# A decoder trunk on one core: where the Conformer's norm is multiplied in, where six key pieces stand, and how layer-norm sums are issued

## The chip, the cores and the metric

The kernel runs on one core of one Trainium2 chip. The metric is the time of one launch in microseconds, taken on the device; the number compared is the median of several runs. Profiles are of one execution each.

## The reference

The model is a trunk of two layers on 512 positions with 1024 channels, in single precision, with cross-attention into 256 memory tokens. Layer 0 is a recurrent and pooling mixer, then cross-attention, then a gated feed-forward net with a causal convolution of width 3. Layer 1 is a Conformer convolution module, then cross-attention and a feed-forward net again. The change lies between the first feed-forward net and the second cross-attention, so it is these lines that matter:

```python
def rms_norm(x, g):
    return x * lax.rsqrt(jnp.mean(x * x, axis=-1, keepdims=True) + EPS) * g

def conformer_conv(x, norm, w1, b1, dw_w, dw_b, ln_g, ln_b, w2, b2):
    h = rms_norm(x, norm) @ w1 + b1            # 1024 -> 2048
    h = jax.nn.glu(h, axis=-1)                 # a * sigmoid(b)
    h = causal_dwconv(h, dw_w, dw_b)           # 31 taps
    h = jax.nn.silu(layer_norm(h, ln_g, ln_b)) # mean and variance over channels
    return h @ w2 + b2

# the second attention's keys depend on the memory alone:
m = rms_norm(mem, mem_norm); k = m @ wk; v = m @ wv
```

## The kernel before

**Layout.** Activations lie with channels on the 128 partitions: `X` is eight tiles of 128x512 (channel block c, all positions). A weight of 1024x1024 is eight pieces of 128x1024, and a piece serves one output block: eight 128x128 blocks, one for each input block.

**Products.** Single precision is made of three products in a reduced format: `mm3` (L158, L159, L160) multiplies high by high, high by low and low by high parts. So an output block of 512 columns is 8 x 3 = 24 matmuls, and one of the memory's 256 columns as well. `load_w` loads a piece by DMA on SyncE (`raw`, three buffers), makes its high part `whi` on ScalarE (L152) and its low part `wlo` by a subtraction on VectorE or, for the Conformer's `pieces` and the values, on GpSimd (L153, `eng=G`). `whi` and `wlo` have four buffers each, so a piece's parts are made when the piece four before it has been used up. `split` does the same for an activation: high part on ScalarE, low part on VectorE.

**Order.** Each engine runs its instructions in a fixed order, which a tile scheduler derives from the order of the code, priorities (`load_w` runs ahead by `AHEAD`), and `issue_after` marks. The whole trunk is one stream of matmuls on TensorE.

**Two ways to apply an RMS norm.** `Norm.feed` (L176 to L185) takes each block as it is finished, multiplies it by the gain alone into an operand's high and low part, and adds up squares. The positions' factor r = 1/sqrt(mean + eps) is only known when all blocks are; whoever uses the product multiplies by r afterwards. `Scaled` only adds up squares in `feed`; `scale()` makes r (`rstd`: a sum over partitions by two matmuls L216, L217, a square root on ScalarE L237, a reciprocal on VectorE L239), and `split(c)` then multiplies block c by gain and r (L209) and splits the product. Before, the Conformer's norm `n3` is a `Norm`.

**The Conformer.** `glu(c)` makes output block c of the two halves: 24 matmuls for the sigmoid's half `psb`, 24 for `psa`, the multiplications by r (L676, L680), the sigmoid (L677), and their product `h` (L683). Four DMAs on SyncE (L690) copy h into a stacked form for the convolution on TensorE. `conv_pe(c)` computes some of the 31 taps by matmuls against diagonal weights, which GpSimd writes just before (L705); the matmuls are L711, and there are 3 groups of 4 taps for the blocks 0 to 6 and 8 groups for block 7. `conv(c)` adds the other taps on VectorE (L729), ScalarE and GpSimd (L727). `quarters` (L223) sums finished blocks over channels for the layer norm: four matmuls of full single precision into four 32-row strips, called after every fourth block for the mean (`mu`) and again for the variance (`var`). Then r, the multiplications L774, the activation, and the second projection `pw2`.

**Keys of the second attention.** `mem.keys(n)` is one weight piece against the memory's 256 columns: 24 matmuls of 256 columns. It depends on nothing in the trunk, and is used as filler. Five of the eight (`KE = 5`) stand in the first feed-forward net, two in each of the steps g = 2 and 3 and one in g = 4, behind `down(g - 1)`. Number 5 stands in the Conformer before `conv_pe(7)`, and numbers 6 and 7 behind the values in the layer norm.

Of the kernel before, what the change touches and what calls it, by code (L numbers as in the profile page):

```python
# [12 lines left out]
AF = mybir.ActivationFunctionType  # L13
ALU = mybir.AluOpType
# [4 lines left out]
C = D // P  # L19
# [12 lines left out]
N_POOL = [4] * 7 + [0]  # L32
LAG = 5

KE = 5
WINDOWS = (2, 4, 8, 16)


# [16 lines left out]
def trunk(ctx: ExitStack, tc: tile.TileContext, I: dict, out: bass.AP):  # L55
    nc = tc.nc
    V, A, G, PE = nc.vector, nc.scalar, nc.gpsimd, nc.tensor
# [14 lines left out]
    def nm(s):  # L72
        uid[0] += 1
        return f"{s}_{uid[0]}"
# [13 lines left out]
    def tmp_f(n=T):  # L88
        return tmp.tile([P, n], F32, tag="tmp", name=nm("tmp"))
# [26 lines left out]
    def col(name, i=0):  # L116
        j = _COL[name] + i
        return par[:, j : j + 1]

    onesf = cpool.tile([P, P], F32, tag="onesf", name="onesf")  # L120
# [16 lines left out]
    def load_w(src=None, eng=None, raw=None, parts=1):  # L137
        with tc.high_priority(0 if raw is not None else AHEAD):
            if raw is None:
                raw = wp.tile([P, D], F32, tag="raw", name=nm("raw"), bufs=3)  # L140
                nc.sync.dma_start(raw, src)
            hi = wp.tile([P, D], F32R, tag="whi", name=nm("whi"))
            lo = wp.tile([P, D], F32R, tag="wlo", name=nm("wlo"))
            n = D // parts
            for i in range(0, D, n):
                split(raw[:, i : i + n], hi[:, i : i + n], lo[:, i : i + n], eng)
        return hi, lo

    def split(src, hi=None, lo=None, eng=None):
        hi = act_r() if hi is None else hi  # L150
        lo = act_r() if lo is None else lo
        A.activation(hi, src, AF.Copy)  # L152
        (eng or V).tensor_tensor(lo, src, hi.bitcast(F32), op=ALU.subtract)  # L153
        return hi, lo
# [67 lines left out]

    def quarters(ps, xs):  # L223

        for j in range(4):
            n = len(xs) - 4 + j
            PE.matmul(ps[32 * j : 32 * j + 32], onesf[:, :32], xs[n], start=n < 4, stop=n >= 4)  # L227

    def total(ps, out):
        f = tmp_f()  # L230
# [11 lines left out]
    def project(w, i, xs):  # L242
        ps = mm_ps()
        for k in range(C):
            mm3(ps, blk(w, k * P), xs[k], k == 0, k == C - 1)
        if Norm.due:
            Norm.due.r = rstd(Norm.due.ss)
            Norm.due = None
        return ps
# [172 lines left out]
    def ffn(layer, norm, nxt, mem=None):  # L422
        ys = {}

        def up(c):
            ps = project(load_w(I["wup"][(layer * 2) * CF + c]), c, norm.x)
            g = tmp_f(T + 2)
            G.memset(g[:, :2], 0.0)  # L428
            V.tensor_tensor(g[:, 2:], ps, norm.r, op=ALU.mult)  # L429
            y = tmp_f()  # L430
            dw = lambda j: col("f_dw_w", (layer * 3 + j) * CF + c)
            A.activation(y, g[:, 2:], AF.Identity, scale=dw(2), bias=col("f_dw_b", layer * CF + c))  # L432
            for j in (1, 0):
                V.scalar_tensor_tensor(y, g[:, j : j + T], dw(j), y, op0=ALU.mult, op1=ALU.add)  # L434
            A.activation(y, y, AF.Gelu_apprx_tanh)  # L435
            G.tensor_tensor(y, y, norm.r, op=ALU.mult)  # L436
            ps = project(load_w(I["wup"][(layer * 2 + 1) * CF + c]), c, norm.x)
            V.tensor_tensor(y, ps, y, op=ALU.mult)  # L438
            ys[c] = split(y)

        def down(g):
            for j in range(C // 2):
                w = load_w(I["wdown"][(layer * NG + g) * (C // 2) + j])
                for i in range(2):
                    n = 2 * j + i
                    ps = mm_ps()
                    for k in range(GC):
                        mm3(ps, blk(w, k * 2 * P + i * P), ys[g * GC + k], k == 0, k == GC - 1)
                    V.tensor_tensor(X[n], X[n], ps, op=ALU.add)  # L449
                    if g == NG - 1:  # L450
                        nxt.feed(n)

        for g in range(NG):
            for c in range(g * GC, (g + 1) * GC):
                up(c)
            if g:
                down(g - 1)
                if mem and g == 1:
                    mem.operand(0)
                    mem.operand(1)  # L460
                    mem.outputs()
                for n in range(2 * g - 4, 2 * g - 2):
                    if mem and 0 <= n < KE:
                        mem.keys(n)
        if nxt:
            down(NG - 1)
        else:
            finish([ys[(NG - 1) * GC + k] for k in range(GC)])
# [196 lines left out]
    def conformer(norm, nxt, mem):  # L665
# [7 lines left out]
        def glu(c, w):  # L673
            psb = project(w[0], c, norm.x)
            b = tmp_f()
            V.tensor_tensor(b, psb, norm.r, op=ALU.mult)  # L676
            A.activation(b, b, AF.Sigmoid, bias=col("c_b_pw1", C + c))  # L677
            psa = project(w[1], c, norm.x)
            a = tmp_f()
            V.tensor_tensor(a, psa, norm.r, op=ALU.mult)  # L680
            h = tmp.tile([P, T + 4], F32, tag="h", name=nm("h"), bufs=3)
            G.memset(h[:, :4], 0.0)
            V.scalar_tensor_tensor(h[:, 4:], a, col("c_b_pw1", c), b, op0=ALU.add, op1=ALU.mult)  # L683
            stacked = [act_f() for _ in range(4)]
            for j in range(4):

                v = h[32 * j : 32 * j + 32, 1 : 1 + T].unsqueeze(1).broadcast_to([32, 4, T])
                dims = [list(d) for d in v.ap]
                dims[1][0] = 1
                nc.sync.dma_start(stacked[j], bass.AP(v.tensor, v.offset, dims))  # L690
            hs[c] = h[:, 4:], stacked
# [58 lines left out]
        for c in range(C):  # L750
            if c < C - 1:
                glu(c + 1, w)
            if c == C - 1:
                mem.keys(KE)
            conv_pe(c)
            if c < C - 2:
                w = pieces(c + 2)
            elif c == C - 1:
                mem.eng = G
                ready = [mem.piece(i) for i in range(3)]  # L760
            conv(c)
# [10 lines left out]
        xs = []  # L772
# [5 lines left out]
        with tc.issue_after(late.ins):  # L778
            mem.values(0, ready)
            mem.values(1)  # L780
            for n in range(KE + 1, C):
                mem.keys(n)
        for n in range(C):
            ps = project(load_w(I["pw2"][n], G), n, xs)
# [5 lines left out]
    mem = Memory(0, load=False)  # L790
# [19 lines left out]
    for n in range(C):  # L810
        mem.keys(n)
        n0.split(n)
    n1, n2, n3 = Norm(("xa_norm", 0)), Norm(("f_norm", 0)), Norm(("c_norm", 0))
    n4, n5 = Norm(("xa_norm", C)), Norm(("f_norm", C))
    mixer(n0, n1)
    attention(0, n1, mem, n2)
    mem = Memory(1)
    ffn(0, n2, n3, mem=mem)
    conformer(n3, n4, mem)
    attention(1, n4, mem, n5)  # L820
    ffn(1, n5, None)


# [65 lines left out]
```

## Time and profile before

| what | us |
|---|---|
| median of three runs | 1503.77 (1503.7 to 1505.58) |
| profiled execution, its own time | 1505.68 |
| its span | 1503.9 |
| TensorE busy | 1481.5 (99%) |
| VectorE / ScalarE / GpSimd busy | 936.2 / 636.5 / 216.6 |

In the trace of before the feed-forward net's last down projection ends near 775, the GLU runs from there to near 883, the layer norm to near 939, and the second projection follows. How to read the rows below: the first number is the start in us from the span's start, the second the duration; then engine, line, operation, output<-inputs, shape and count, and in brackets the time for which the engine stood idle before it and whose end released it. Each row of TensorE with `xN` is N records in a row; a convolution or layer-norm sum in full single precision leaves two records for each instruction.

### The profile page before, as it was taken

To read this page: it belongs to the slowest core of one execution; us is meant where nothing else is said; L and a number is where in the kernel's file an instruction comes from. 1 tells how busy PE (TensorE), PEld (TensorE's weight loads), DVE (VectorE), ACT (ScalarE), POOL (GpSimd) and SP (SyncE) were. 2 spreads that over 40 slices of the span, in tenths; PEclk is the share of its full clock that TensorE was granted. 3 is DMA by queue.
4 is the path that set the end of the run, shared out by engine and by line. 5 is a ranking of instruction groups with operands and counts; after the bars stand their busy time and mean duration, and the time that the engine had idled before them with its cause. 6 is when DMAs were issued, how large, how long until landed. Compare 5 with 4: busy or idle time off the path is not lost.

```text
span 1503.9 us, 17839 instructions
## 1 busy us (share of the span) xinstructions
PE 1481.5 (99%) x6974; PEld 1210.1 (80%) x6974; DVE 936.2 (62%) x1222; ACT 636.5 (42%) x878; POOL 216.6 (14%) x226
## 2 busy tenths in 40 slices
PE   8999999999999999999999999999999999999997
PEld 7888788888888888888877665888888888888886
DVE  7987765656554555555566996866665554545556
ACT  7578744444432333333253336544443332323333
POOL 0011300000110101000036763300001010101000
PEclk9999999999999999999999999999999999999998
DMA  7432332213333332333326542331233333323321
GB/s 273 149 108 85 121 118 97 71 31 124 98 98 98 96 107 94 111 98 105 94 81 169 158 141 94 103 94 57 71 98 98 98 98 98 98 96 92 97 81 57
DMA packets 47477, 156.24 MB, mean 104 GB/s; under 512 B 5280, under 2 KB 7328, under 8 KB 47392
## 3 DMA queue, kind: packets, MB, share of 16 engines
q1 hardware_dynamic: 46160, 154.03, 33.1%
q8 instruction: 55, 0.90, 0.2%
q10 hardware_dynamic: 1232, 1.06, 0.2%
q14 instruction: 30, 0.25, 0.1%
HBM read 144.58 MB, written 2.10 MB: 98 GB/s over the span
## 4 chain that ended last, share of the span: by engine, by line
PE 89%; DVE 5%; issue 2%; ACT 2%; POOL 1%; DMA 1%; SPq 0%; DVEq 0%; POOLq 0%; ACTq 0%
PE mm L159 27%; PE mm L158 27%; PE mm L160 27%; PE aux L711 2%; PE aux L160 1%; PE aux L159 1%; PE aux L158 1%; DVE wlo L153 1%; ACT whi L152 1%; DVE act L177 1%; POOL tmp L569 1%; PE aux L372 0%; DVE r L239 0%; DVE actf L774 0%; PE aux L227 0%
## 5 line engine op out<-in xcount | busy, mean ns | idle before, releaser
L159 PE MATMUL mm<-act,whi 128*128 128x512 f32 (+1 forms) x1845 | 712.8, 387 | 3.1 <-DVE act L153 1.9
L160 PE MATMUL mm<-act,wlo 128*128 128x512 f32 (+1 forms) x1845 | 712.5, 386 | 1.6 <-DVE wlo L153 1.6
L158 PE MATMUL mm<-act,whi 128*128 128x512 f32 (+1 forms) x1845 | 712.4, 387 | 0.7 <-ACT act L176 0.5
L152 ACT ACTIVATE whi<-raw 128x1024 fp32r<-128x1024 f32 x267 | 282.7, 1060 | 617.0 <-PE mm L159 460.8
L159 PEld LDWEIGHTS mm<-act,whi 128*128 128x128 f32 x1845 | 347.4, 188 | 77.0 <-issue 3.3
L160 PEld LDWEIGHTS mm<-act,wlo 128*128 128x128 f32 x1845 | 347.3, 188 | 73.7 <-DVE wlo L153 2.4
L158 PEld LDWEIGHTS mm<-act,whi 128*128 128x128 f32 x1845 | 347.5, 188 | 72.0 <-ACT act L176 1.0
L153 DVE TENSOR_TENSOR wlo<-raw,whi 128x1024 fp32r<-128x1024 f32 x233 | 288.0, 1238 | 60.5 <-ACT whi L152 60.0
L436 POOL TENSOR_TENSOR tmp<-tmp,r 128x512 f32<-128x512 f32 x48 | 62.0, 1292 | 652.0 <-ACT tmp L435 647.1
L449 DVE TENSOR_TENSOR x<-x,mm 128x512 f32<-128x512 f32 x88 | 60.4, 687 | 99.8 <-PE mm L160 99.8
L429 DVE TENSOR_TENSOR tmp<-mm,r 128x512 f32<-128x512 f32 x48 | 33.2, 692 | 124.1 <-PE mm L160 124.1
L153 POOL TENSOR_TENSOR wlo<-raw,whi 128x1024 fp32r<-128x1024 f32 x34 | 82.8, 2435 | 114.4 <-ACT whi L152 114.4
L438 DVE TENSOR_TENSOR tmp<-mm,tmp 128x512 f32<-128x512 f32 x48 | 33.2, 691 | 95.5 <-POOL tmp L428 80.9
L729 DVE SCALAR_TENSOR_TENSOR aux<-h,par,aux 128x496 f32<-128x496 f32 (+14 forms) x105 | 75.1, 728 | 8.2 <-PE aux L711 6.0
L153 DVE TENSOR_TENSOR act<-tmp,act 128x512 fp32r<-128x512 f32 x102 | 73.3, 723 | 5.9 <-ACT act L152 5.7
L152 ACT ACTIVATE act<-tmp 128x512 fp32r<-128x512 f32 x102 | 63.8, 628 | 26.4 <-DVE tmp L185 7.6
L434 DVE SCALAR_TENSOR_TENSOR tmp<-tmp,par,tmp 128x512 f32<-128x512 f32 x96 | 71.9, 749 | 1.7
L435 ACT ACTIVATE tmp<-tmp 128x512 f32<-128x512 f32 x48 | 30.3, 632 | 95.1 <-DVE tmp L434 95.1
L428 POOL MEMSET tmp<- 128x2 f32 x48 | 4.6, 99 | 300.0 <-DVE tmp L185 300.0
L177 DVE SCALAR_TENSOR_TENSOR act<-x,par,act 128x512 fp32r<-128x512 f32 x40 | 40.2, 1008 | 8.0 <-ACT act L176 8.0
L432 ACT ACTIVATE tmp<-tmp,par 128x512 f32<-128x512 f32 x48 | 38.6, 805 | 0.6 <-DVE tmp L429 0.6
L239 DVE RECIPROCAL r<-tmp 128x512 f32<-128x512 f32 (+1 forms) x10 | 28.7, 2872 | 15.5 <-ACT tmp L237 15.5
(195 smaller groups left out, 1234.8 us busy)
## 6 DMA issues: line engine op xcount, KB each, us to landing
raw<-in_wup SPq DMA_DIRECT2D x96, 512.0 KB, 3.5
raw<-in_wdown SPq DMA_DIRECT2D x48, 512.0 KB, 3.5
raw<-in_pw SPq DMA_DIRECT2D x24, 512.0 KB, 3.6
raw<-in_win SPq DMA_DIRECT2D x20, 512.0 KB, 3.6
raw<-in_wv SPq DMA_DIRECT2D x16, 512.0 KB, 4.8
raw<-in_wk SPq DMA_DIRECT2D x16, 512.0 KB, 3.9
raw<-in_wq SPq DMA_DIRECT2D x16, 512.0 KB, 3.6
raw<-in_wo SPq DMA_DIRECT2D x16, 512.0 KB, 3.6
```

What stands on the lines that cost most here:

```text
L152: A.activation(hi, src, AF.Copy)
L153: (eng or V).tensor_tensor(lo, src, hi.bitcast(F32), op=ALU.subtract)
L158: PE.matmul(ps, wh, xh, start=first, stop=False)
L159: PE.matmul(ps, wh, xl, start=False, stop=False)
L160: PE.matmul(ps, wl, xh, start=False, stop=last)
L177: self.last = V.scalar_tensor_tensor(lo, X[c], g, hi.bitcast(F32), op0=ALU.mult, op1=ALU.subtract)
L429: V.tensor_tensor(g[:, 2:], ps, norm.r, op=ALU.mult)
L432: A.activation(y, g[:, 2:], AF.Identity, scale=dw(2), bias=col("f_dw_b", layer * CF + c))
L434: V.scalar_tensor_tensor(y, g[:, j : j + T], dw(j), y, op0=ALU.mult, op1=ALU.add)
L436: G.tensor_tensor(y, y, norm.r, op=ALU.mult)
L449: V.tensor_tensor(X[n], X[n], ps, op=ALU.add)
L729: V.scalar_tensor_tensor(ps[:, s:], h[:, : T - s], tap(s, c), ps[:, s:], op0=ALU.mult, op1=ALU.add)
```

## The change

There are three edits. The first makes `n3` a `Scaled`, and moves keys: none are left in the feed-forward net, two stand behind it, two behind the making of r, one after four of the operand's blocks and one after all eight; `KE` is 6, so that numbers 6 and 7 stay where they were. The second follows from it: `glu` needs no factor r, so the sigmoid and the product read PSUM. The third marks three of the four matmuls of `quarters` to be issued after the one that is created first, which takes the last of the four blocks.

```diff
     def quarters(ps, xs):
-        for j in range(4):
+        def quarter(j):
             n = len(xs) - 4 + j
-            PE.matmul(ps[32 * j : 32 * j + 32], onesf[:, :32], xs[n], start=n < 4, stop=n >= 4)
+            return PE.matmul(ps[32 * j : 32 * j + 32], onesf[:, :32], xs[n], start=n < 4, stop=n >= 4)
+
+        with tc.issue_after(quarter(3).ins):
+            for j in range(3):
+                quarter(j)
...
-                for n in range(2 * g - 4, 2 * g - 2):
-                    if mem and 0 <= n < KE:
-                        mem.keys(n)
...
             b = tmp_f()
-            V.tensor_tensor(b, psb, norm.r, op=ALU.mult)
-            A.activation(b, b, AF.Sigmoid, bias=col("c_b_pw1", C + c))
+            A.activation(b, psb, AF.Sigmoid, bias=col("c_b_pw1", C + c))
             psa = project(w[1], c, norm.x)
-            a = tmp_f()
-            V.tensor_tensor(a, psa, norm.r, op=ALU.mult)
...
-            V.scalar_tensor_tensor(h[:, 4:], a, col("c_b_pw1", c), b, op0=ALU.add, op1=ALU.mult)
+            V.scalar_tensor_tensor(h[:, 4:], psa, col("c_b_pw1", c), b, op0=ALU.add, op1=ALU.mult)
...
-            if c == C - 1:
-                mem.keys(KE)
             conv_pe(c)
...
-            for n in range(KE + 1, C):
+            for n in range(KE, C):
                 mem.keys(n)
...
-    n1, n2, n3 = Norm(("xa_norm", 0)), Norm(("f_norm", 0)), Norm(("c_norm", 0))
+    n1, n2, n3 = Norm(("xa_norm", 0)), Norm(("f_norm", 0)), Scaled(("c_norm", 0))
...
     ffn(0, n2, n3, mem=mem)
+    mem.keys(0)
+    mem.keys(1)
+    n3.scale()
+    mem.keys(2)
+    mem.keys(3)
+    for c in range(C):
+        n3.split(c)
+        if c % 4 == 3:
+            mem.keys(4 + c // 4)
     conformer(n3, n4, mem)
```

Later lines move by a few numbers: what was L239 is L244 after the change, L306 (the keys' product with the memory's factor) L311, L683 is L682, L711 is L710. TensorE has the same number of instructions as before, VectorE eight fewer.

The order on VectorE where the Conformer begins, before. `x` are the channel blocks, `mm_6069` the last down product, `act` the parts of the operand, `r_6139` the factor, `h` the first GLU blocks:

```order
L449 TENSOR_TENSOR x<-x,mm_6069 128x512
L177 SCALAR_TENSOR_TENSOR act_6084<-x,par,act_6083 128x512
L185 TENSOR_TENSOR tmp_6089<-tmp_6067,tmp_6087 128x512
L153 TENSOR_TENSOR act_6131<-tmp_6089,act_6130 128x512
L239 RECIPROCAL r_6139<-tmp_6137 128x512
L676 TENSOR_TENSOR tmp_6141<-mm_6105,r_6139 128x512
L680 TENSOR_TENSOR tmp_6169<-mm_6144,r_6139 128x512
L683 SCALAR_TENSOR_TENSOR h_6171<-tmp_6169,par,tmp_6141 128x512
```

The same place after the change, from the reciprocal on. `bigr` are parts of the keys, `mm_5964` and `mm_5999` key products:

```order
L244 RECIPROCAL r_5956<-tmp_5954 128x512
L311 TENSOR_TENSOR tmp_5989<-mm_5964,r_271 128x256
L311 TENSOR_TENSOR tmp_6024<-mm_5999,r_271 128x256
L209 SCALAR_TENSOR_TENSOR tmp_6028<-x,par,r_5956 128x512
L153 TENSOR_TENSOR bigr_3951<-tmp_5989,bigr_3950 128x256
L153 TENSOR_TENSOR bigr_3951<-tmp_6024,bigr_3950 128x256
L209 SCALAR_TENSOR_TENSOR tmp_6034<-x,par,r_5956 128x512
L153 TENSOR_TENSOR act_6031<-tmp_6028,act_6030 128x512
L209 SCALAR_TENSOR_TENSOR tmp_6040<-x,par,r_5956 128x512
L209 SCALAR_TENSOR_TENSOR tmp_6046<-x,par,r_5956 128x512
L153 TENSOR_TENSOR act_6037<-tmp_6034,act_6036 128x512
```

Between the reciprocal and the first `h` VectorE now has 24 instructions (eight L209, eight splits of them, four key products and four splits of those) where it had two.

On TensorE, keys 0 and 1, the two statistic matmuls and keys 2 to 5 stand in this order ahead of GLU 0. The two halves of GLU 0 are not one after the other: ten products of `psb` come first, then single or a few products of `psa` and `psb` in turn, and last thirteen of `psa`, so that the eighth operand block is first asked for late among the 48.

The order on TensorE at the last convolution block, before. `aux_6990` is block 6, `aux_7068` block 7; the `mm_7231` and `mm_7232` rows are the second attention's values:

```order
L160 MATMUL mm_7039<-bigr_3940,wlo_7036 128x256
L227 MATMUL stat_6182<-actf_6771,onesf 32x512
L158 MATMUL mm_7231<-whi_7107,bigr_3930 128x512
...
L160 MATMUL mm_7232<-whi_7107,bigr_3931 128x512
L711 MATMUL aux_6990<-actf_6861,actf_6991 32x512
...
L711 MATMUL aux_6990<-actf_6864,actf_6991 32x504
L158 MATMUL mm_7231<-whi_7113,bigr_3930 128x512
...
L159 MATMUL mm_7231<-wlo_7120,bigr_3940 128x512
L711 MATMUL aux_7068<-actf_6982,actf_7069 32x512
```

After the change, `aux_7010` is block 6 and `aux_7053` block 7; `mm_6974` is the last GLU product, `mm_7216` and `mm_7217` are values:

```order
L160 MATMUL mm_6974<-act_6107,wlo_6916 128x512
L158 MATMUL mm_7216<-whi_7092,bigr_3930 128x512
...
L159 MATMUL mm_7217<-wlo_7099,bigr_3930 128x512
L710 MATMUL aux_7010<-actf_6884,actf_7011 32x512
...
L710 MATMUL aux_7010<-actf_6887,actf_7011 32x504
L710 MATMUL aux_7053<-actf_7002,actf_7054 32x512
```

The key piece (`mm_7039`) and the layer-norm sum are gone from here; 17 value matmuls stand between the last GLU product and block 6 (12 before, behind the key piece), and none between block 6 and block 7, where there were 20.

For the blocks 1 to 5 the convolution of block c stood four matmuls into the `psa` half of GLU c+2. Block 1, before (`mm_6436` is the end of `psb` of GLU 3, `mm_6464` the start of its `psa`, `aux_6381` the convolution):

```order
L160 MATMUL mm_6436<-act_6083,wlo_6399 128x512
L158 MATMUL mm_6464<-act_5913,whi_6404 128x512
L159 MATMUL mm_6464<-act_5914,whi_6404 128x512
L160 MATMUL mm_6464<-act_5913,wlo_6405 128x512
L158 MATMUL mm_6464<-act_5933,whi_6404 128x512
L711 MATMUL aux_6381<-actf_6253,actf_6382 32x512
```

After the change, block 0 shows what now holds for all of them (`mm_6353` is `psb` of GLU 2, `aux_6299` the convolution):

```order
L160 MATMUL mm_6353<-act_6089,wlo_6317 128x512
L158 MATMUL mm_6353<-act_6095,whi_6316 128x512
L159 MATMUL mm_6353<-act_6096,whi_6316 128x512
L710 MATMUL aux_6299<-actf_6215,actf_6300 32x512
```

The convolution of block c now stands 17 matmuls into `psb` of GLU c+2, eleven earlier than before for the blocks 1 to 5.

More of the change, by code (lines that the diff above doesn't have):

```diff
@@ L33 @@
 LAG = 5
-KE = 5
+KE = 6
 WINDOWS = (2, 4, 8, 16)
```

## The prediction

> **What bounds the kernel now.** I read the page's engine line first, then the busy time by stretch, then the rows of TensorE around the places that the change touches.
>
> ```profile
> PE 1481.5 (99%) x6974; PEld 1210.1 (80%) x6974; DVE 936.2 (62%) x1222; ACT 636.5 (42%) x878; POOL 216.6 (14%) x226
> 500.00:600.00 100.00, 100.00 (x465) 83.81 (x464) 54.22 (x66) 33.45 (x40) 7.99 (x12) 1.00 0.32 100
> 755.00:784.00 29.00, 26.47 (x107) 20.73 (x106) 20.29 (x22) 14.67 (x21) 11.68 (x5) 0.94 0.29 85
> 784.00:905.00 121.00, 120.04 (x647) 80.90 (x646) 102.29 (x137) 43.32 (x56) 77.78 (x59) 1.00 0.54 150
> 905.00:945.00 40.00, 38.44 (x162) 24.02 (x158) 25.37 (x34) 28.44 (x40) 14.56 (x6) 0.96 0.25 79
> ```
>
> TensorE is busy for 99% of the span. The other rows give the stretch, its length, the busy time of TensorE, of its weight loads, VectorE, ScalarE and GpSimd, and the granted clock. In the feed-forward net, where five key pieces now stand, no gap is left, so they hide nothing there and leave without cost. The change issues the same matmuls as before, so its effect lies in gaps and half-clock periods, and the three other stretches hold 2.53, 0.96 and 1.56 us of gaps.
>
> First the boundary to the Conformer:
>
> ```profile
> 769.67 0.39 PE L160 MATMUL mm<-act,wlo 128*128 128x512 f32 x1
> ...
> 774.43 0.39 PE L160 MATMUL mm<-act,wlo 128*128 128x512 f32 x1
> 775.37 0.49 PE L158 MATMUL mm<-act,whi 128*128 128x512 f32 x1 [0.55 <-ACT act L176]
> 777.09 0.50 PE L159 MATMUL mm<-act,whi 128*128 128x512 f32 x1 [1.23 <-DVE act L177]
> ...
> 779.67 0.63 PE L158 MATMUL mm<-act,whi 128*128 128x512 f32 x1
> ...
> 782.24 0.52 PE L158 MATMUL mm<-act,whi 128*128 128x512 f32 x1
> 931.18 0.28 PE L158 MATMUL mm<-bigr,whi 128*128 128x256 f32 x1
> ...
> 936.81 0.28 PE L160 MATMUL mm<-bigr,wlo 128*128 128x256 f32 x1
> 939.39 0.71 PE L159 MATMUL mm<-act,whi 128*128 128x512 f32 x1 [1.45 <-DVE act L153]
> ...
> 942.89 0.42 PE L158 MATMUL mm<-act,whi 128*128 128x512 f32 x1
> ```
>
> Starts count, since records overlap. From 769.67 to 774.43 are 21 steps of 0.227 us. These 21 matmuls are the first seven blocks of GLU 0, so the last down projection ends one step behind 769.67, at E = 769.9. Then the eighth block's parts are late, made by ScalarE and VectorE, and after these gaps six matmuls, 779.67 to 782.24, run at 0.43 us each: the clock was halved. Key matmuls of 256 columns take 0.12 us (47 steps from 931.18 to 936.81), so a key piece is 24 x 0.12 = 2.9 us.
>
> **The change part by part.** A plus is time added.
>
> *What the boundary loses now.* From E to 782.24 are 12.3 us, in which 24 + 6 products and two statistic matmuls run: 32 x 0.227 = 7.3. It loses 5.1 us, and with keys as cover all of that can go: **-5.1**.
>
> *What the boundary gets.* After E come keys 0 and 1 (to E+5.8), two statistic matmuls (E+6.3), and keys 2 to 5 (E+17.9). Then GLU 0 wants the new operand, one of eight blocks each three matmuls, and ends its `psb` 5.4 us and both halves 10.9 us later, at E+28.8 if nothing is late. When are the blocks there?
>
> ```profile
> 779.96 1.28 ACT L237 ACT_TABLE_LOAD   x1 [0.71 <-PE stat L217]
> 781.25 0.69 ACT L237 ACTIVATE tmp<-stat,eps 128x512 f32<-128x512 f32 x1
> 781.97 3.35 DVE L239 RECIPROCAL r<-tmp 128x512 f32<-128x512 f32 x1 [2.95 <-ACT tmp L237]
> 47.73 0.74 DVE L209 SCALAR_TENSOR_TENSOR tmp<-x,par,r 128x512 f32<-128x512 f32 x1
> 48.39 0.42 DVE L306 TENSOR_TENSOR tmp<-mm,r 128x256 f32<-128x256 f32 x1
> 48.72 0.74 DVE L209 SCALAR_TENSOR_TENSOR tmp<-x,par,r 128x512 f32<-128x512 f32 x1
> 49.38 0.68 DVE L153 TENSOR_TENSOR act<-tmp,act 128x512 fp32r<-128x512 f32 x1
> 49.98 0.42 DVE L153 TENSOR_TENSOR bigr<-tmp,bigr 128x256 fp32r<-128x256 f32 x1
> 50.32 0.68 DVE L153 TENSOR_TENSOR act<-tmp,act 128x512 fp32r<-128x512 f32 x1
> ```
>
> The statistic is there at E+6.4; the table load and square root take 1.28 + 0.69 us behind some ScalarE work on a weight piece (about 0.8), so to E+9.2, and the reciprocal 3.35, to E+12.5. The rows from 47.73 on, of the first layer, show the same building of an operand between keys: from start to start 0.66 us for L209, 0.60 for its split, 0.33 for a key product and 0.34 for that one's split. Eight, eight, four and four of them are 13 us, one after the other on VectorE: the last block stands at about E+25.5, a block every 1.6 us from E+14. TensorE asks for the first block at E+17.9, when it is done, and then for a new one every 1.4 us, as the order takes both halves of GLU 0 in turn. Putting these times into the order, matmul by matmul, I get gaps of 0.1 us in sum.
>
> What speaks for a larger loss is that two engines' instructions hold each other:
>
> ```profile
> 945.54 5.20 POOL L153 TENSOR_TENSOR wlo<-raw,whi 128x1024 fp32r<-128x1024 f32 x2 [10.36 <-ACT whi L152]
> 946.01 2.48 DVE L153 TENSOR_TENSOR act<-tmp,act 128x512 fp32r<-128x512 f32 x1 [0.77 <-ACT act L152]
> 948.41 2.61 DVE L153 TENSOR_TENSOR bigr<-tmp,bigr 128x256 fp32r<-128x256 f32 x1
> L683 DVE SCALAR_TENSOR_TENSOR h<-tmp,par,tmp x8: 751/1888/2669, 789.6 to 884.6; 128x512 f32<-128x512 f32 x8
> ```
>
> While GpSimd split two pieces, a VectorE split that takes 0.68 took 2.48, and one that takes 0.42 took 2.61: each ended with a GpSimd instruction. The eight L683, minimum, median and maximum in ns, vary from 751 to 2669 for the same reason. Three GpSimd splits of Conformer pieces (the second of GLU 0 and both of GLU 1, 2.4 us or more each) come due in the window from E+12.5, since their buffers come free as the keys' pieces are used up. Nearly every VectorE instruction there reads two tensors of SBUF (x and r, or a product and its high part). With three holds, each from the start of a split that falls on a waiting VectorE instruction, the same exercise puts the low parts of blocks 0, 1 and 3 to E+20.7, 22.7 and 27.4 and the last to E+32.4. TensorE then waits 2.7, 1.3 and 2.8 us for the three and 0.5 for others: 7.2, and GLU 0 ends at E+36.0, not 28.8. At the half clock that such gaps leave, the products between them take 0.43, which fills part of the later gaps but lengthens the end: 8.3 to 9.3. I take **+8.9**; the ends are 0.1 and 9.3.
>
> The Trainium skill, "SBUF — State Buffer", section "Who interferes with whom", states that a VectorE instruction with two SBUF inputs contends with a GpSimd instruction that reads SBUF, and that the one that comes first has the shared ports for its whole instruction. The rows of 945.54 to 948.41 agree. By the same page the new `h`, which reads PSUM and one SBUF tensor, is no longer held; that is off TensorE's path except for the waits below.
>
> *Queues.* Six key pieces of 512 KB in 18 us are 175 GB/s on SyncE's queue; the stretch from 784 on moves 150 at a share of 0.54, so that is 0.63, and I cost it at nothing. ScalarE and VectorE split them ahead of the reciprocal, at 1.1 and 1.2 us for each 2.9 of TensorE; the bound above nothing is one late piece, the 1.2.
>
> *Convolutions.* `conv_pe(c)` now stands 17 matmuls (3.9 us) behind the end of `psa` of GLU c+1; for c = 1 to 5 it was 28 (6.4 us).
>
> ```profile
> 811.40 1.06 ACT L152 ACTIVATE whi<-raw 128x1024 fp32r<-128x1024 f32 x1 [3.38 <-PE mm L159]
> 812.54 2.41 POOL L153 TENSOR_TENSOR wlo<-raw,whi 128x1024 fp32r<-128x1024 f32 x1 [3.07 <-ACT whi L152]
> 814.91 1.29 POOL L705 TENSOR_TENSOR actf<-fold,par 128x384 f32<-128x384 f32 x1
> 801.29 0.85 POOL L705 TENSOR_TENSOR actf<-fold,par 128x384 f32<-128x384 f32 x1
> ```
>
> The taps are made on GpSimd behind the split of a piece whose high part waits for TensorE to use up `psa`'s piece: 1.06 + 2.41 + 0.85 = 4.3 and some 0.1 between, 4.4 us. So TensorE waits about 0.55 at each of six blocks, 3.3 in sum. The whole stretch from 784 to 905 has 0.96 us of gaps now, of which I put 0.2 to these places: **+3.1**. With 1.29 for the taps the waits would be 1.0 each, +5.8; if the pieces are split before this, 0.
>
> *Sums.*
>
> ```profile
> 914.18 1.47 PE aux L227 x4
> 916.31 0.97 PE aux L227 x2
> 918.18 0.97 PE aux L227 x2
> 920.75 0.98 PE aux L227 x4
> 885.84 1.05 PE L227 MATMUL stat<-actf,onesf 128*32 128x512 f32 x2
> 898.20 6.89 PE L711 MATMUL aux<-actf,actf 128*32 128x512 f32 x64 [0.24 <-DVE actf L738]
> ```
>
> A group takes 0.97 us whether it is one instruction (x2 records) or two, since the strips run side by side. Before, the order has eleven groups; after, five (one is still split in 3 and 1). One of the six saved lies ahead of the last GLU product: **-1.0**. The other five count in the tail, next.
>
> *The tail.* Before the sum at 885.84 stand the 24 matmuls of key number 5, 2.9 us, so the last GLU product ends at Q = 882.9. From there to the first `pw2` matmul, whose wait ends at 939.39, are 56.5 us. Number 5 leaves (it was paid for at the boundary): 53.5. Five groups fewer are 4.9, and the tail's gaps of today (1.56 and 0.24 by the rows above, and some more) about 2.1: TensorE has 46.5 us to do. But the convolution of block 7 started at 898.20, Q+15.3, behind number 5, a sum, 32 value products and block 6. Now 17 value products (3.9), a wait of 0.55 and block 6 (24 records against 64 in 6.89 us, 2.6) are ahead of it: Q+7.0. It needs the copies of h.
>
> ```profile
> 887.02 4.28 SPq L690 DMA_DIRECT2D actf<-h  x4
> DMA to landing us min/median/max: 3.8/5.0/5.5
> ```
>
> h is there some 0.9 us after Q (one instruction, 0.75 us unheld by the L683 row), four issues take 4.28 us, and the last lands 3.8 to 5.5 us after its issue: Q+9 to Q+10.7. I take Q+9.9, so TensorE waits 2.9 us. The matmuls from 939.39 to 942.89 show what follows a gap of 1.45: eight in 3.5 us in place of 1.8, so 1.5 more. The tail is 46.5 + 2.9 + 1.5 = 50.9 against 53.5: **-2.6**; the ends are -7.0 (copies in time) and 0. As a test by the other side: block 7's start to 939.39 is a chain of 41.2 us, from which the five groups take up to 4.9; behind Q+9.9 that ends between Q+46.2 and Q+51.1.
>
> On the half clock, the Trainium skill, "TensorE: Matmul & The Clock Gate", Part 1, states that the clock falls only after at least one whole idle window, some 3.4 us. The trace differs: eight slow matmuls follow a gap of 1.45 us.
>
> *Sum:* -5.1 + 8.9 + 3.1 - 1.0 - 2.6 = **+3.3**, on 1505.68 of the profiled execution 1509.0. That execution stands 1.9 over the median of 1503.77, so I forecast 1507.1.
>
> **The rivals.** *Operands not held* (the other side). If the three GpSimd splits are done before E+12.5, or fall between VectorE's instructions, the boundary loses 0.1 and not 8.9: 1498.3, faster. For it: GpSimd is idle for 17 of the 29 us from 755 on, and a split waits only for a buffer. Against: those buffers come free only as the keys are used up. It decides from where fewer than two splits fall into the window.
>
> *Copies in time.* If SyncE has nothing else in front and the copies land by Q+7.0, the tail gives -7.0: 1502.7, no change. For it: the smallest landing, 3.8. Against: the issues alone take 4.28.
>
> *More waits in the convolutions.* Each of the six waits grows from 0.55 to 1.0 and the copies land at Q+12: +2.7 and +2.1, 1511.9 and above. For it: the 1.29 row, and that the stretch's DMA share is 0.54 already, with pieces loaded while h is copied.
>
> *No half clock.* If gaps of about 3 us leave the clock alone, as that page of the Trainium skill would have it, the boundary loses 1.5 and the tail 1.5 less: 1504.1, no change. Against: the rows at 779.67 and 939.39.
>
> *The change does not do what it says*, in that the order hardly moves: it does move, and this gets 0.02.
>
> **How the numbers follow.** Differences under 0.2%, 3.0 us, can hardly be told from no change. The forecast has 0.42, and as it lies at that bound, 0.29 of it slower and 0.13 same. More waits 0.15, slower. Copies in time 0.14: 0.10 same, 0.04 faster. No half clock 0.05, same. Not held 0.22: 0.19 faster, 0.03 same. No effect 0.02, same. That makes faster 0.23, same 0.33, slower 0.44. The range, 1498.0 to 1513.0, takes in the upper half of the unheld case and the lower half of the added waits, so that some 0.18 is left out; the forecast's own is 1503 to 1510.
>
> **What would show it.** Right: on TensorE a trickle of waits for VectorE's L153 in GLU 0, 8 to 9 us in all, with L209 and L153 rows of over 2 us beside GpSimd's splits; six waits of half a microsecond before L710, released by GpSimd; before block 7 a wait of 2 to 3 us on a DMA; five groups of L232. Wrong: GLU 0 without waits, no wait for the copies, or gaps in the feed-forward net where the keys stood.

## The result, and the profile after

| kernel | median, us (range, runs) | ratio to before [95% interval] |
|---|---|---|
| before | 1505.26 (1501.82 to 1507.35, 20) | 1 |
| changed | 1505.88 (1504.19 to 1508.19, 20) | 1.0007 [1.0, 1.0014] |

The change makes no difference that 20 runs against 20 could tell. On these runs the median of before is 1.5 us above the three that the forecast started from. The profiled execution of the changed kernel took 1505.71 us, with the same span as before, 1503.9.

Inside, it is another program. TensorE's rows from the boundary to the next attention, after the change (times count from the span's start; the idle time and its releaser are in brackets):

```profile
754.79 0.28 PE L158 MATMUL mm<-bigr,whi 128*128 128x256 f32 x1
...
772.51 0.39 PE L158 MATMUL mm<-act,whi 128*128 128x512 f32 x1
775.09 0.66 PE L159 MATMUL mm<-act,whi 128*128 128x512 f32 x1 [2.19 <-DVE act L153]
777.01 0.80 PE L159 MATMUL mm<-act,whi 128*128 128x512 f32 x1 [0.42 <-DVE act L153]
781.33 0.50 PE L159 MATMUL mm<-act,whi 128*128 128x512 f32 x1 [1.67 <-DVE act L153]
...
789.88 0.39 PE L160 MATMUL mm<-act,wlo 128*128 128x512 f32 x1
805.39 2.76 PE L710 MATMUL aux<-actf,actf 128*32 128x512 f32 x24 [0.39 <-POOL actf L721]
...
877.57 2.76 PE L710 MATMUL aux<-actf,actf 128*32 128x512 f32 x24 [0.39 <-POOL actf L721]
887.44 0.39 PE L158 MATMUL mm<-whi,bigr 128*128 128x512 f32 x1
891.85 4.29 PE L710 MATMUL aux<-actf,actf 128*32 128x512 f32 x30 [0.39 <-POOL actf L704]
896.59 6.87 PE L710 MATMUL aux<-actf,actf 128*32 128x512 f32 x58 [0.45 <-DMA actf<-h]
936.82 0.50 PE L159 MATMUL mm<-act,whi 128*128 128x512 f32 x1 [2.11 <-DVE act L153]
947.92 0.50 PE L159 MATMUL mm<-act,whi 128*128 128x512 f32 x1 [1.91 <-DVE act L153]
989.36 0.39 PE L216 MATMUL stat<-act,ones 128*128 128x512 f32 x1
```

The first row is E, key 0 behind the last down product (before, E is 769.9, as the prediction works out, and not the 775 given with the profile of before). The keys run without a gap to 772.51, where the statistic had its late parts before. Then GLU 0 waits three times for VectorE's splits, the convolutions of the blocks 0 to 5, and that of block 6 in the tail, wait 0.39 us each for GpSimd (L721 is a small memset that GpSimd runs right behind the taps of L704), Q is 887.44, and the second projection waits twice where it waited once. The last row is the next attention's statistic, at 989.62 before. Between these marks:

| stretch | before | after | of it keys moved | difference | forecast |
|---|---|---|---|---|---|
| E to the end of GLU 0 | 16.6 | 35.3 | +17.3 (six) | +1.5 | -5.1 + 8.9 |
| to Q | 96.4 | 97.3 | | +0.9 | +3.1 - 1.0 |
| Q to the product behind the first wait of `pw2` | 56.5 | 49.4 | -2.9 (one) | -4.2 | -2.6 |
| from there to the next statistic | 50.2 | 52.5 | | +2.3 | none |
| sum | | | | +0.5 | +3.3 |

Five keys' time came out of the feed-forward net, which still has no gap, and the rest of the program differs by under 1 us. What lay behind the waits in GLU 0 is on VectorE's rows and on GpSimd's in the same microseconds, first VectorE:

```profile
764.08 3.35 DVE L244 RECIPROCAL r<-tmp 128x512 f32<-128x512 f32 x1 [0.74 <-ACT tmp L242]
768.61 5.16 DVE L153 TENSOR_TENSOR bigr<-tmp,bigr 128x256 fp32r<-128x256 f32 x2
777.82 2.86 DVE L209 SCALAR_TENSOR_TENSOR tmp<-x,par,r 128x512 f32<-128x512 f32 x1
```

and GpSimd:

```profile
765.14 2.41 POOL L153 TENSOR_TENSOR wlo<-raw,whi 128x1024 fp32r<-128x1024 f32 x1 [53.47 <-ACT whi L152]
768.02 5.47 POOL L153 TENSOR_TENSOR wlo<-raw,whi 128x1024 fp32r<-128x1024 f32 x2 [0.47 <-ACT whi L152]
777.38 2.75 POOL L153 TENSOR_TENSOR wlo<-raw,whi 128x1024 fp32r<-128x1024 f32 x1 [3.90 <-ACT whi L152]
```

The reciprocal, with one input, runs beside the first split in its usual 3.35 us. Two key splits that take 0.34 each need 5.16 beside the next two, and one L209 of 0.66 needs 2.86 beside the last.

### The profile page after: what moved, and what is told of

It reads as the page before. It is cut to its first block, busy times and chain, and to the rows that moved or that the text cites. A ratio compares the mean times of both kernels' runs of the same rounds, so it can differ in the third digit from the quotient of the medians.

```text
span 1503.9 us, 17834 instructions
## 1 busy us (share of the span) xinstructions
PE 1475.2 (98%) x6974; PEld 1209.2 (80%) x6974; DVE 928.9 (62%) x1214; ACT 634.6 (42%) x878; POOL 214.9 (14%) x226
## 5 line engine op out<-in xcount | busy, mean ns | idle before, releaser
L152 ACT ACTIVATE act<-tmp 128x512 fp32r<-128x512 f32 x110 | 68.9, 629 | 34.5 <-DVE tmp L209 9.5
L153 DVE TENSOR_TENSOR act<-tmp,act 128x512 fp32r<-128x512 f32 x110 | 78.8, 721 | 5.4 <-ACT act L152 5.0
L244 DVE RECIPROCAL r<-tmp 128x512 f32<-128x512 f32 (+1 forms) x10 | 28.7, 2872 | 9.3 <-ACT tmp L242 9.3
L177 DVE SCALAR_TENSOR_TENSOR act<-x,par,act 128x512 fp32r<-128x512 f32 x32 | 30.2, 947 | 1.6 <-ACT act L176 1.6
```

## The experiments

Each was timed against the kernel before on the same chip. What was measured is given as the median in us and the ratio to before with its 95% interval.

**Is it the hold?** Theory: GpSimd's splits hold VectorE's instructions with two SBUF inputs. Rival: VectorE's own 24 instructions are too slow. The low parts of four pieces are filled by an instruction that reads nothing:

```diff
-                split(raw[:, i : i + n], hi[:, i : i + n], lo[:, i : i + n], eng)
+                if zero:
+                    A.activation(hi[:, i : i + n], raw[:, i : i + n], AF.Copy)
+                    G.memset(lo[:, i : i + n].bitcast(F32), 0.0)
+                else:
+                    split(raw[:, i : i + n], hi[:, i : i + n], lo[:, i : i + n], eng)
...
-            return load_w(I["pw1"][C + c], G), load_w(I["pw1"][c], G)
+            return load_w(I["pw1"][C + c], G, zero=c < 2), load_w(I["pw1"][c], G, zero=c < 2)
```

> The changed kernel, but the low parts of the four weight pieces of GLU 0 and 1 are filled with zeros by a GpSimd memset, which reads nothing, and no longer made by a GpSimd subtraction (so the low-part products of these four pieces are left out of the result). Theory, holds: the three waits in GLU 0 (2.2, 0.4 and 1.7 us, and the half clock behind them, 6.7 us in all) come from VectorE instructions with two SBUF inputs that are held by GpSimd's splits; the long VectorE rows of 2.5 us go, the waits go, and the kernel is 5.5 to 6.7 us faster than the changed one, near 1499.5 where before is 1505.3. Rival, build: VectorE's own 24 instructions are too slow for TensorE; the waits stay at 4 us or more and the time is that of the changed kernel within 1.5 us.

Measured: 1498.38, 0.9957 [0.9944, 0.9971], a span 6.6 us shorter than the changed kernel's. The rows of VectorE, GpSimd and TensorE at the place (code lines are four higher here: L157 is the split, L162 and L164 are products):

```profile
769.17 0.76 DVE L157 TENSOR_TENSOR bigr<-tmp,bigr 128x256 fp32r<-128x256 f32 x2
767.53 0.96 POOL L148 MEMSET wlo<- 128x1024 f32 x1 [1.93 <-PE mm L164]
773.07 0.40 PE L162 MATMUL mm<-act,whi 128*128 128x512 f32 x1
```

The same two key splits take 0.76, and GLU 0 runs from 773.07 without one wait. The build was never too slow; the hold is shown. From E to the first convolution are 44.3 us here and 50.6 in the changed kernel, so at this place it is worth 6.3 us; the medians differ by 7.5.

**The same without leaving work out.** The four pieces are split on VectorE:

```diff
-            return load_w(I["pw1"][C + c], G), load_w(I["pw1"][c], G)
+            e = V if c < 2 else G
+            return load_w(I["pw1"][C + c], e), load_w(I["pw1"][c], e)
```

> The changed kernel with the four pieces of GLU 0 and 1 split on VectorE, not on GpSimd; everything is computed. Theory, holds: no hold is left, but VectorE has four splits of 1.24 us more, two or three of them ahead of the last operand, which then stands 2.5 to 3.7 us later than E+25.5; the loss of GLU 0 falls from 6.7 to 1 to 4 us, so 3 to 5 us faster than the changed kernel, near 1502. Rival, build: VectorE is the limit, the four splits lengthen it by 5 us and the kernel is 3 to 5 us slower than the changed one.

Measured: 1498.77, 0.9959 [0.9946, 0.9971]. Better than either number expected: TensorE has no gap between the keys and the first convolution, although VectorE has 5 us more to do there. The first row below is VectorE's, two of the splits in 2.35 us between operands; the second TensorE's next gap.

```profile
776.94 2.35 DVE L153 TENSOR_TENSOR wlo<-raw,whi 128x1024 fp32r<-128x1024 f32 x2
799.48 2.76 PE L711 MATMUL aux<-actf,actf 128*32 128x512 f32 x24 [0.34 <-POOL actf L722]
```

**The sums alone**, on the kernel before: the edit of `quarters` and nothing else.

> The kernel before with the issue of the layer-norm sums alone changed. Theory, TensorE's time: six groups of 0.97 us fewer; one of them ahead of the last GLU product and most of the others on the chain from block 7 to the second projection, so 4 to 6 us faster than before, near 1500. Rival, hidden: the tail is a chain of VectorE and ScalarE work behind block 7, in which a sum only waits for the last block anyway; then 1 us from the first sum, and the wait ahead of the second projection grows from 1.45 by what the sums save: within 2 us of before.

Measured: 1502.96, 0.9982 [0.9974, 0.9991]. Between the two numbers: of 5.8 us some 2.1 to 2.7 are left. The rows of TensorE ahead of the second projection, then VectorE's multiplications by r (L779, L774 before) and GpSimd's splits:

```profile
931.71 0.73 PE L158 MATMUL mm<-act,whi 128*128 128x512 f32 x2 [1.56 <-ACT act L152]
935.30 0.80 PE L159 MATMUL mm<-act,whi 128*128 128x512 f32 x1 [2.85 <-DVE act L153]
925.35 9.29 DVE L779 TENSOR_TENSOR actf<-actf,r 128x512 f32<-128x512 f32 x8
925.63 5.46 POOL L153 TENSOR_TENSOR wlo<-raw,whi 128x1024 fp32r<-128x1024 f32 x2 [0.32 <-ACT whi L152]
```

Seven of the eight multiplications in the kernel before:

```profile
932.23 6.50 DVE L774 TENSOR_TENSOR actf<-actf,r 128x512 f32<-128x512 f32 x7
```

The waits there are 4.41 us and not 1.45. The eight multiplications, which read two SBUF tensors, took 9.29 us beside two splits, where seven took 6.50 before, beside one: the sums come earlier, and so do the multiplications, into the splits. About half of what the sums save is given back there; how much of that is the hold is tested below, with r in PSUM.

**The sums taken out of the changed kernel again:**

> The changed kernel with the sums issued as before (each of the four matmuls as its block is ready). Theory, chain: in the tail what the sums save on TensorE is partly given back as waits ahead of the second projection, as the sums alone did on the kernel before (0.9982, 2.7 us, of six groups of 0.97); so 2 to 3.5 us slower than the changed kernel, near 1508.5. Rival, TensorE's time: with key number 5 gone from the tail nothing covers a sum, and the full six groups come back: 5 to 6 us slower, near 1511.5.

Measured: 1509.27, 1.0033 [1.0021, 1.0046], against 1.0007 with them: 0.26%, 3.9 us. It lies between the two theories and nearer to the chain; the wait ahead of `pw2` is one of 2.87 us here, and the second, of 1.91, is not there.

**Cover without the operand.** On the kernel before only keys 0 and 1 are moved:

```diff
-                    if mem and 0 <= n < KE:
+                    if mem and 2 <= n < KE:
...
     ffn(0, n2, n3, mem=mem)
+    mem.keys(0)
+    mem.keys(1)
```

> The kernel before with keys 0 and 1 alone moved from the feed-forward net to directly behind it; the norm is applied as before and so are the sums. Theory: two key pieces, 5.8 us of TensorE work, cover the 2.5 us by which the last operand parts and the statistic are late, with no operand to be built; the waits at the boundary and their half clock go, 5.1 us, near 1500.2. Rival, cover was needed where the keys were: the feed-forward net, which has no gap now, gets gaps of 1 us or more at the two places, or the wait moves to the first GLU products; within 2 us of before.

Measured: 1500.56, 0.9972 [0.9961, 0.9984]. The statistic follows the products without a wait, and the feed-forward net has no gap (first TensorE's row, then the net's stretch, with TensorE busy for all of its 240 us):

```profile
775.23 0.39 PE L216 MATMUL stat<-act,ones 128*128 128x512 f32 x1
500.00:740.00 240.00, 240.00 (x1095) 200.20 (x1094) 126.69 (x153) 76.95 (x91) 18.58 (x26) 1.00 0.33 99
```

So the boundary's 4 to 5 us can be had with two keys and the norm left as it was. The hold is here too: VectorE's last addition for the statistic (L185, at 769.28) takes 2.88 us and not 0.68, beside a GpSimd split that runs from 769.13. The keys cover it, and TensorE does not wait.

**Both parts on the kernel before:**

> The kernel before with keys 0 and 1 moved behind the feed-forward net and with the sums issued four together; the norm stays applied behind the products. Theory: the two gains lie in different stretches and add, 0.9972 x 0.9982 = 0.9954, 1498.1 where before is 1505.0. Rival: the sums' gain hangs on when GpSimd splits the pieces of the second projection, and moves with any shift; then 1496 to 1500.5.

Measured: 1496.49, 0.9949 [0.9936, 0.9962]; they add, within the interval. The rival's range takes the time in as well, but the waits did not move: they are 1.56 and 2.83 us ahead of and in `pw2`, as with the sums alone.

**The hold in the layer norm.** To those two, r is written to PSUM:

```diff
-        r = scale_of(total(var, stat_ps()))
+        r, sd = total(var, stat_ps()), tmp_f()
+        A.activation(sd, r, AF.Sqrt, bias=eps)
+        V.reciprocal(r, sd)
```

> The kernel before with keys 0 and 1 moved and the sums four together, and besides with the layer norm's factor r written to PSUM, so that the eight multiplications by r on VectorE read one tensor of SBUF and one of PSUM. Theory, holds: with the sums alone these eight took 9.29 us beside two GpSimd splits, against 6.5 on the kernel before; unheld they take 6.5 or less, the waits ahead of the second projection (1.56 and 2.85 us with the sums alone) shrink by 2.3 to 3 us, and the kernel is 2 to 4 us faster than the one without this edit, near 1495.5. Rival, port: VectorE is as slow on PSUM or is held in any case; the multiplications stay at 9 us beside the splits and the time stays within 1 us.

Measured: 1494.2, 0.9931 [0.9918, 0.9944], 2.3 us less. VectorE's eight multiplications, and GpSimd's split in the same time:

```profile
920.01 4.86 DVE L781 TENSOR_TENSOR actf<-actf,stat 128x512 f32<-128x512 f32 x8
920.29 2.42 POOL L153 TENSOR_TENSOR wlo<-raw,whi 128x1024 fp32r<-128x1024 f32 x1 [0.33 <-ACT whi L152]
938.00 0.50 PE L159 MATMUL mm<-act,whi 128*128 128x512 f32 x1 [1.44 <-DVE act L153]
```

4.86 us for eight and not 9.29, beside such splits: moving one input to PSUM ends the hold, and GpSimd keeps its work. Of TensorE's waits the one of 1.56 stays, the one of 2.83 is gone, and one of 1.44 comes 8 us later in `pw2`, behind an operand's split of 2.45 us beside the next GpSimd split. Gone too is the half clock that stood behind the wait of 2.83 (in the run without this edit the matmuls from 930.34 to 933.32 stand 0.43 us apart). The Trainium skill, "SBUF — State Buffer", section "Who interferes with whom", says that a VectorE instruction with at most one SBUF input, outside the modes that use two ports, does not contend with GpSimd; this pair of runs agrees.

**The taps first.** On the changed kernel, GpSimd writes the taps of a block ahead of the splits that they stood behind, by building them before the GLU of the next block and with a higher priority:

```diff
             if c < C - 1:
+                made[c, 0] = make_taps(c, 0)
                 glu(c + 1, w)
...
         def conv_pe(c):
...
+                taps = made.pop((c, at), None)
+                if taps is None:
+                    taps = make_taps(c, at)
```

> The changed kernel with the taps of blocks 0 to 6 written by GpSimd a block earlier, so that they stand ahead of the two piece splits on GpSimd's queue. Theory: the six or seven waits of 0.39 us ahead of the convolutions come from the taps behind the split, and go: 2.3 to 2.7 us faster than the changed kernel, near 1503.3, if nothing else is late there. Rival: the waits only change their releaser (the copies of h, or the split itself, which the value or GLU products then wait for), and the time stays within 1 us.

Measured: 1508.3, 1.002 [1.0012, 1.0029], some 2 us slower than the changed kernel, with intervals that just touch. The waits ahead of the convolutions are gone, as expected; but the scheduler now puts the convolutions 17 matmuls earlier. Up to Q the kernel gains 1.2 us, and from Q to the next statistic it loses 3.3: block 7 still waits for the copies of h, and `pw2` waits for its weights, first for a high part from ScalarE and then for a low part from GpSimd:

```profile
891.99 1.02 PE L720 MATMUL aux<-actf,actf 128*32 128x512 f32 x2 [0.46 <-DMA actf<-h]
938.78 0.50 PE L158 MATMUL mm<-act,whi 128*128 128x512 f32 x1 [2.80 <-ACT whi L152]
941.21 0.80 PE L160 MATMUL mm<-act,wlo 128*128 128x512 f32 x1 [1.70 <-POOL wlo L153]
```

The cause of the waits is shown. What they alone are worth is not, since the order moved with them.

**Key number 5 back** ahead of block 7's convolution, in the changed kernel:

```diff
-        if c % 4 == 3:
-            mem.keys(4 + c // 4)
+        if c == 3:
+            mem.keys(4)
...
+            if c == C - 1:
+                mem.keys(5)
             conv_pe(c)
```

> The changed kernel with key number 5 back ahead of the convolution of block 7, so that five pieces stand at the boundary and not six. Theory: GLU 0 ends when VectorE has its operands, which does not depend on a key piece in front of it, so the waits there grow by the 2.9 us of the piece; in the tail the piece covers the wait of block 7 on the copies of h (about 2.1 us from its first records to the fourth copy), so it costs there 2.9 - 2.1: the whole within -1 to +2 us of the changed kernel, 1505 to 1508. Rival, the key is free work that only has to be done somewhere: 2.9 us less at the boundary and 2.9 more in the tail with the copies still waited for, no change at the copies; or the tail, bound by the chain behind block 7, takes it for nothing, 2 to 3 us faster, near 1503.

Measured: 1498.66, 0.9953 [0.994, 0.9965]: 7 us less than the changed kernel. Both expectations fell. TensorE's waits in GLU 0, then VectorE's rows, then GpSimd's, and last the wait in `pw2`:

```profile
771.58 1.36 PE L158 MATMUL mm<-act,whi 128*128 128x512 f32 x3 [1.88 <-ACT act L152]
776.89 0.50 PE L159 MATMUL mm<-act,whi 128*128 128x512 f32 x1 [0.57 <-DVE act L153]
764.33 3.34 DVE L244 RECIPROCAL r<-tmp 128x512 f32<-128x512 f32 x1
768.20 2.66 DVE L209 SCALAR_TENSOR_TENSOR tmp<-x,par,r 128x512 f32<-128x512 f32 x1
765.04 2.40 POOL L153 TENSOR_TENSOR wlo<-raw,whi 128x1024 fp32r<-128x1024 f32 x1 [0.92 <-ACT whi L152]
938.53 0.50 PE L160 MATMUL mm<-act,wlo 128*128 128x512 f32 x1 [1.25 <-POOL wlo L153]
```

I had taken the operand's time as given. But with a key piece less in front, the GLU pieces get their buffers a piece earlier: two of GpSimd's four splits are over before VectorE's reciprocal ends, one of them beside it, and two holds are left at the operand (a third falls on a key's split at 761.98, and the reciprocal behind it is only 0.25 us later than in the changed kernel). From E to the first convolution are 45.9 us (50.6 in the changed kernel), 2.9 of that the key itself. In the tail key 5 is 2.9 us more, yet the stretch from Q to the next statistic is 99.9 and not 101.9: the copies are no longer waited for, and the two waits ahead of and in `pw2` shrink to 0.23, 0.22 and 1.25. How much of this belongs to the copies and how much to the holds that shift with it was not separated.

**The changed kernel unheld**: its four pieces on VectorE and r in PSUM.

> The changed kernel with the four pieces of GLU 0 and 1 split on VectorE and with the layer norm's r written to PSUM. Theory, holds: the first edit took 6 to 7 us from the changed kernel (1498.8), the second shortens the eight multiplications by the hold that is in them (7.14 us against 4.86 unheld) and with that the wait of 2.11 us ahead of the second projection: another 1.5 to 2.5 us, 1496.5. Rival: the wait there is set by ScalarE's activations (0.8 us each beside splits of 0.6), which stay; within 0.7 us of 1498.8.

Measured: 1494.96, 0.9929 [0.9917, 0.9942], against 0.9959 with the first edit alone. That is 3.8 us by the medians, more than either expectation. Of the two waits in `pw2`, 2.11 and 1.92 with the first edit alone, one of 1.30 is left:

```profile
938.38 0.50 PE L159 MATMUL mm<-act,whi 128*128 128x512 f32 x1 [1.30 <-DVE act L153]
```

The expectation had left out the half clock: with the first edit alone eight matmuls from 942.77 on stand about 0.43 us apart, some 1.5 us in all, and here none do.

**The second projection's pieces on VectorE**, on the version with r in PSUM:

> The kernel before with keys 0 and 1 moved, the sums four together and the layer norm's r in PSUM, and besides with all eight pieces of the second projection split on VectorE. Theory, holds: one hold is left in the tail (a split of an operand, 2.45 us beside a GpSimd split), behind which TensorE waits 1.44 us; it goes, but three splits of 1.24 us come ahead of the last operand on VectorE. Between 1 us faster and 1 us slower than without this edit (1494.2). Rival, VectorE is the bound of the tail: 3 us slower or more.

Measured: 1493.67, 0.9921 [0.9907, 0.9934], against 0.9931 with overlapping intervals: as expected, no clear difference.

**One more piece of cover.** To that, key 4 moves from the feed-forward net to keys 6 and 7:

> The kernel before with keys 0 and 1 behind the feed-forward net, the sums four together, r in PSUM and the second projection's pieces split on VectorE, and besides with key number 4 moved from the feed-forward net to the end of the layer norm, beside 6 and 7. Theory, cover: TensorE has four waits of 1.55, 0.22, 0.23 and 0.75 us ahead of and in the first products of the second projection, with a half clock behind them; 2.9 us of key work in front of them takes the place of most: 2 to 3.5 us faster than without this edit (1493.7), near 1491. Rival: one more key product and its split on VectorE and one more piece on GpSimd and ScalarE push the operands back by as much; within 1 us of 1493.7.

Measured: 1491.68, 0.9914 [0.9901, 0.9928]. It has the lowest median of all kernels run. The step is 2.0 us by the medians and 1.0 by the ratios, whose intervals overlap. Ahead of and in `pw2` one wait is left:

```profile
926.27 0.47 PE L158 MATMUL mm<-act,whi 128*128 128x512 f32 x1 [1.39 <-DVE bigr L331]
```

## Why the prediction was right, and where it was not

The time, 1505.88, lies in the range and 1.2 us below the forecast of 1507.1, with a before that itself measured 1.5 higher. The likeliest case read "slower by 3.3", and what came is "no change"; its weight was on the wrong side of the bound. That the time came so near is in part luck: against before the miss is 2.7 us, of which the higher before hid 1.5. And within the stretches of the table, three forecasts were too high, by 2.3, 1.2 and 1.6 us, and a wait that the sum did not have gave 2.3 back.

**The boundary now, -5.1:** about right. The cover-only run took 4 to 5 us by moving keys alone. The hold was already part of this loss: TensorE's wait of 1.23 us at 777.09 was for a VectorE instruction (L177, at 775.35) that took 1.69 us beside a GpSimd split, and 0.75 for the block before it.

**The operand held, +8.9:** the mechanism was right, in the order in which it was forecast (waits of 2.2, 0.4 and 1.7 us for 2.7, 1.3 and 2.8; GLU 0's end at E+35.3 for E+36.0 to 38). The term measured 6.6 if all of the 5.1 went, and 6.3 by the run without holds. The half clock was charged to all of it; it came in one spell of 3.4 us from the first gap on, over the second, and not behind the third.

**The convolutions, +3.1:** the waits were there, at all six places and released by GpSimd, at 0.39 us for 0.55. With the sums, which came as the five groups that were forecast, the stretch gave +0.9 for +2.1.

**The tail, -2.6:** it measured -4.2. The wait for the copies was mis-sized: the sum lets block 7 start when the last of the four has landed. Block 7's matmuls go through the four copies in turn, so the first ones started on the first copy. SyncE's issues in the changed kernel:

```profile
888.83 4.20 SPq L689 DMA_DIRECT2D actf<-h  x4
```

The fourth matmul's wait ended at 896.59, Q+9.2 for the forecast of Q+9.9. Block 7's 64 records take from about 894.5 to 903.5, 2.0 us longer than the 6.9 of before, and no half clock follows; I had 2.9 and 1.5. Two more errors met here. The sum took the wait ahead of `pw2` out with the gaps of before, and it was there, 2.11 us. And TensorE's own work was about 1.6 us less than the 46.5 of the sum: 49.4 without the waits of 0.39, 2.0 and 2.11 us is 44.9.

**What was left out, +2.3:** the second wait in `pw2`. The prediction had seen that VectorE's last splits stand beside GpSimd's there, since it quoted those rows of before, but used them only for the boundary. VectorE's and GpSimd's rows of the changed kernel:

```profile
942.26 2.49 DVE L153 TENSOR_TENSOR act<-tmp,act 128x512 fp32r<-128x512 f32 x1 [0.77 <-ACT act L152]
944.67 2.59 DVE L153 TENSOR_TENSOR bigr<-tmp,bigr 128x256 fp32r<-128x256 f32 x1
941.79 5.19 POOL L153 TENSOR_TENSOR wlo<-raw,whi 128x1024 fp32r<-128x1024 f32 x2 [9.79 <-ACT whi L152]
```

Before, a held key split stood behind the last operand; now it stands ahead of it, so the hold reaches TensorE.

**The rivals.** "Operands not held" did not come, but its price was about right: with the hold taken away the kernel is 6.6 us faster than before by the medians of that run, where 5.5 was forecast. "No half clock" was half right: the clock fell behind some gaps and not behind others (below). That key 5 was better where it stood was not among the cases; putting it back took 7 us off.

## What to carry to other kernels

When work moves, list which VectorE instructions with two SBUF inputs will now run in the same microseconds as GpSimd's reads, at the new place and at every later one that shifts with it: each meeting cost about 2 us here, and a gain elsewhere was in part given back through it. One input in PSUM, or the piece split on VectorE itself, removed it without moving anything. Cover is best taken from where nothing waits: two keys at the boundary gave what six and a new operand did not.

## What the runs showed that was not expected

The half clock. Gaps of about 2 us were followed by slow matmuls in some places and not in others. In the changed kernel the product behind a gap of 2.11 us and those after it ran at full clock, with 0.24 us from start to start; behind the gap of 1.91 they did so for 1.5 us, and then slowed:

```profile
936.82 0.50 PE L159 MATMUL mm<-act,whi 128*128 128x512 f32 x1 [2.11 <-DVE act L153]
937.16 0.40 PE L160 MATMUL mm<-act,wlo 128*128 128x512 f32 x1
937.40 0.40 PE L158 MATMUL mm<-act,whi 128*128 128x512 f32 x1
...
947.92 0.50 PE L159 MATMUL mm<-act,whi 128*128 128x512 f32 x1 [1.91 <-DVE act L153]
...
949.46 0.63 PE L160 MATMUL mm<-act,wlo 128*128 128x512 f32 x1
```

The slow spells at 775.09 here and at 939.39 before lasted 3.4 and 3.5 us. The Trainium skill, "TensorE: Matmul & The Clock Gate", Part 1, gives the clock's window as some 3.4 us and as running freely, not from the kernel's start. The spells' length and their late beginning agree with that; that a window must be idle for all of its length does not, since the gaps were 1.5 to 2.2 us. A half clock behind a short gap is better priced as a chance than as a certainty.
